# Attention units and projection steps: steps handed out by the units' key blocks instead of by their number

## The chip, the core and the metric

The kernel runs on one core of a Trainium2 chip. The metric is the device time of one execution in microseconds (us); the time before is the median of three runs. A profile is one execution taken by the hardware profiler. TensorE stands in it as PE (matmuls) and PEld (weight loads), VectorE as DVE, ScalarE as ACT, GpSimd as POOL, SyncE, which only issues transfers, as SP.

## The reference

Two decoder layers over 1024 tokens of width 1024, all in float32. Layer 0 mixes with native sparse attention (8 heads in two groups) and differential attention (4 heads, two softmax maps each); layer 1 with stick-breaking attention (16 heads). After each mixer comes an output projection, and then a SwiGLU of hidden width 2816.

```python
o_nsa  = nsa_mixer(q, kc, vc, ks, vs, kw, vw, gates, ...)   # compressed + selected + window, gated
o_diff = diff_mixer(q, k, v, ...)     # (softmax1 - lam * softmax2) @ v, RMSNorm per head
x = x + concat(o_nsa, o_diff) @ w_out;      x = x + swiglu(rmsnorm(x))
# layer 1, strictly causal:
log_rest = where(strict, log_sigmoid(-z), 0);  suffix = cumsum_from_the_right(log_rest) - log_rest
o = exp(log_sigmoid(z) + suffix) @ v;       x = x + o @ w_out;   x = x + swiglu(rmsnorm(x))
out = rmsnorm(x)
```

## The kernel before

Every projection is computed from a high and a low part of both operands, three matmuls for one (mm3, lines 126 to 128). Attention is cut into **units**, each a query block of one head or pair of heads, and a unit into stages s0 (stack the queries), s1 (scores, mask, softmax or scan), s2 (transpose the weights, multiply by the values, store) and, in differential attention, s3 (transpose the result, line 616). `run_segments` pushes the units of a segment one after the other: as unit u comes in, its s0 is written, s1 of the unit before it, s2 of the one before that. Behind each push it writes some **steps** of the projections that the next segment needs. A step is the work up to a generator's `yield`: one token block of a projection (24 matmuls of 256 columns), half a chunk of a query or key projection of layer 1 (12 of 512), or one block of the early output projection (18 of 256). A segment has a number of units, a list of generators, a total of steps n, the number of first units that get none (skip), and in the two last ones a fifth number, 30, over which the steps are spread while n is 1000 (no limit, so what is left goes behind the last unit). Before the change, the steps given out are proportional to the units passed.

The segments: sparse attention group 0 (unit names n0..) with 14 steps, group 1 (n1..) with 17; differential heads d0 to d2 with 9, 17 and 19, and d3 with 30 and four empty units at its end; stick-breaking pairs of heads b0 to b7, eight units each (b712 is pair 7, second head, query blocks 4 and 5; b713 blocks 6 and 7), with 8 steps for even pairs (12 for b6), 16 for odd ones and 30 for b7, which has two empty units at its end. Key blocks of a unit grow with its query block: 1 to 8 in a differential head, 3, 7, 11, 15 in a stick-breaking head, where a unit has two query blocks.

`OutProj.early` writes the output projection of the first six of eight inner blocks during the last segment: per block (oao.. in layer 0, obo.. in layer 1, the digits are column chunk and token block) a read of the residual into a staging tile xr (line 729), 18 matmuls, an add (735) and a write (736). Layer 0 has 8 staging tiles, layer 1 has 4. `late` adds the last two inner blocks (oaq, obq, weights oax, obx) and reads the rows back (750); these rows f0x, f1x go into the norm of the feed-forward (f0n0v, f0n0y and so on, line 180), for which DVE does most of the work. The last head's result reaches the late projection by `put_last` (692, 693).

The program is not executed in the order in which it is written: a scheduler of the build reorders the instructions of each engine by a timeline of its own, within what tiles and pools allow, and each engine then executes its list strictly in that order.

Of the kernel before, what the change touches and what calls it, by code (L numbers as in the profile page):

```python
# [39 lines left out]
def trunk(ctx: ExitStack, tc: tile.TileContext, x, norm_mix, norm_ffn, norm_final,  # L40
# [191 lines left out]
    def run_segments(segs):  # L232
        pend = []

        def push(u):
            pend.append(u)
            for st in range(4):
                for d in range(min(len(pend), 6)):
                    v = pend[-1 - d]
                    if v and v[st] and v[4][st] == d:  # L240
                        v[st]()

        for units, fills, n, skip, *spread in segs:
            work = list(fills)
            taken = 0

            def step():
                while work:
                    try:
                        next(work[0])  # L250
                        return True
                    except StopIteration:
                        work.pop(0)
                return False

            for i, u in enumerate(units):
                push(u)
                want = -(-(spread or [n])[0] * (i + 1 - skip) // max(1, len(units) - skip))
                while taken < want and step():
                    taken += 1  # L260
            while (not units or taken < n) and step():
                taken += 1
        for _ in range(5):
            push(None)
# [5 lines left out]
    def even_attention(op):  # L270
# [220 lines left out]
        def nsa_units(g, q, ks, vs, kw, vw):  # L491
            ap = at_

            def unit(qb, p, box, sel):
                nm = f"n{g}{qb}{p}" + ("s" if sel else "w")
                kb0 = 0 if sel else max(0, qb - 4)
                nk = (qb - kb0 + 1) * 128
# [48 lines left out]
                                                    tmp[:, i * 128:(i + 1) * 128], op=ALU.add)  # L546
                        nc.sync.dma_start(oT_d[g * 2 + p, :, qb * 128:(qb + 1) * 128], os_)

                return s0, s1, s2, None, (0, 1, 2, 3)

            out_ = []
            for qb in range(NT):
                for p in range(2):
                    box = {}
                    out_.append(unit(qb, p, box, False))
                    out_.append(unit(qb, p, box, True))
            return out_

        def diff_units(hd, q, k, v):
            ap = at_  # L560

            def unit(qb):
                nm = f"d{hd}{qb}"
                nk = (qb + 1) * 128
# [56 lines left out]
                    nc.scalar.copy(os_, t[:, :128])  # L621
                    nc.sync.dma_start(oT_d[4 + hd, :, qb * 128:(qb + 1) * 128], os_)

                return s0, s1, s2, s3, (0, 1, 2, 4)

            return [unit(qb) for qb in range(NT)]

        compress()
# [30 lines left out]
        def two(chunk):  # L659
            for _ in range(2):  # L660
                next(chunk)
                yield

        run_segments([
            ([], [fill_kv("ks", [(KS0, 256)], True, lone), fill_kv("kw", [(KW0, 256)], True, lone), two(q0)], 0, 0),
            (nsa(0), [q0, fill_q("q1", NQ0 + 256)], 14, 0),
# [392 lines left out]
    def sb_attention(h, op):  # L1059
        w_in = odd_w_in[0]  # L1060
        with pool("sv", 2) as sv_, pool("sq", 2) as sq, pool("sa", 2) as sa:
# [47 lines left out]
            def unit(i, hh, c):  # L1109
# [63 lines left out]
                    else:  # L1173
                        nc.sync.dma_start(o2T_d[i, pr, c * 256:(c + 1) * 256], tmp[pr])

                return s0, s1, s2, None, (0,1,2,3)

            segs = [([], [v_chunk(0, lone), qk_chunk(0, lone)], 0, 0)]
            xr = []
# [6 lines left out]
            for i in range(8):  # L1186
                units = [unit(i, hh, c) for hh in range(2) for c in range(NT // 2)]
                if i == 7:
                    segs.append((units + [None] * 2, [op.rest(), early], 1000, 2, 30))
                elif i % 2 == 1:  # L1190
                    segs.append((units, [v_chunk((i + 1) // 2), qk_chunk(i + 1)], 16, 2))
                elif i == 6:
                    early = op.early(qk_chunk(i + 1, None, True), 4, stage)
                    segs.append((units, [early], 12, 2))
                else:
                    segs.append((units, [qk_chunk(i + 1)], 8, 2))
            run_segments(segs)

    op = OutProj(oT_d, even_w_out[0], x_d, x1_d, "oa")
# [70 lines left out]
```

## Time and profile before

| | |
|---|---|
| time, median of 3 runs | 2801.74 us (2797.72 to 2805.55) |
| profiled execution: its time, its span | 2809.49 us, 2807.7 us |
| PE busy | 2668.3 us, 95% of the span |
| DVE, ACT, POOL busy | 1880.9, 1244.9, 525.6 us |
| mean granted TensorE clock | 0.981 |

The span runs from the first to the last instruction; the execution's own time is 1.79 us longer. A busy PE counts from issue to modelled end, and matmuls overlap in it. Times in the trace are from the span's start. Attention of layer 0 lies between about 109 and 772 us, its feed-forward until 1460, attention of layer 1 between 1511 and 2110, and then the second feed-forward.

### The profile page before, as it was taken

The numbers are of one execution on the slowest core, as the hardware profiler recorded it, in microseconds if no ns is written. First come the engines' busy times: TensorE is split into PE (matmuls) and PEld (weight loads), VectorE is DVE, ScalarE is ACT, GpSimd is POOL, SyncE is SP. The second block draws the span as 40 slices with busy tenths as digits, with TensorE's granted clock in tenths as the row PEclk, the third lists the DMA queues.
The fourth block names the chain that finished last, engine by engine and source line by source line (L and its number), as shares of the span: only waits on it lengthen the run. The fifth ranks groups of instructions, "written<-read, shape, count | busy, mean of one in ns | idle before, by whom it ended". The sixth has DMA issues, their size and how long they took to land.

```text
span 2807.7 us, 42453 instructions
## 1 busy us (share of the span) xinstructions
PE 2668.3 (95%) x15596; PEld 2307.8 (82%) x15596; DVE 1880.9 (67%) x3266; ACT 1244.9 (44%) x2603; POOL 525.6 (19%) x637
## 2 busy tenths in 40 slices
PE   8999999999979999999999999999887999999998
PEld 7889888898967888888887888787786788888887
DVE  7467667556586666657554767877848657665755
ACT  4366666544353333334443545554425333333433
POOL 3465655444120000000022020211102000000000
PEclk9999999999989999999999999999998999999999
DMA  5100000013445555577643233324434545556754
GB/s 157 32 23 7 23 21 22 23 45 95 123 175 176 150 163 166 159 224 240 198 162 87 59 83 69 94 68 110 124 102 166 174 153 167 160 158 212 256 186 141
DMA packets 327904, 347.70 MB, mean 124 GB/s; under 512 B 24560, under 2 KB 280208, under 8 KB 327696
## 3 DMA queue, kind: packets, MB, share of 16 engines
q1 hardware_dynamic: 327696, 344.98, 40.5%
q8 instruction: 124, 2.03, 0.3%
q14 instruction: 84, 0.69, 0.1%
HBM read 223.79 MB, written 95.94 MB: 114 GB/s over the span
## 4 chain that ended last, share of the span: by engine, by line
PE 69%; DVE 13%; DMA 9%; issue 4%; ACT 4%; POOL 2%; SPq 1%; DVEq 0%; POOLq 0%; ACTq 0%
PE f0o L128 2%; PE f0o L126 2%; PE f0o L127 2%; PE f1o L128 2%; PE f1o L126 2%; PE f1o L127 2%; PE sqo L126 2%; PE sqo L127 2%; PE sqo L128 2%; DMA f1t<-in_ffn_w_down_dram 1%; PE svo L126 1%; PE svo L128 1%; PE svo L127 1%; DMA t_d<-f1t 1%; PE oao L127 1%
## 5 line engine op out<-in xcount | busy, mean ns | idle before, releaser
L113 POOL TENSOR_SCALAR sv0h<-sv0r 128x1024 fp32r<-128x1024 f32 x2 | 2.1, 1057 | 598.9 <-DVE f0c L1043 595.2
L167 POOL TENSOR_TENSOR nf0r<-nf0v,mhalf 128x1 f32<-128x1 f32 x1 | 0.6, 553 | 600.6 <-DVE nf0v L165 600.6
L208 PEld LDWEIGHTS <-ident_b 128*128 128x128 bf16 x352 | 34.2, 97 | 48.2 <-issue 35.7
L1043 DVE TENSOR_TENSOR f1c<-f1o,f1c 128x512 f32<-128x512 f32 x56 | 36.0, 687 | 30.2 <-PE f1o L128 30.1
L1043 DVE TENSOR_TENSOR f0c<-f0o,f0c 128x512 f32<-128x512 f32 x56 | 36.0, 684 | 18.8 <-PE f0o L128 18.8
L951 DVE TENSOR_TENSOR f1t<-f1t 128x256 f32<-128x256 f32 x22 | 9.4, 425 | 51.0 <-DMA f1t<-in_ffn_w_down_dram 51.0
L951 DVE TENSOR_TENSOR f0t<-f0t 128x256 f32<-128x256 f32 x22 | 9.4, 425 | 50.2 <-DMA f0t<-in_ffn_w_down_dram 50.2
L1072 ACT CAST sv<-svo 128x128 fp32r<-128x128 f32 x64 | 17.0, 268 | 48.7 <-PE svo L128 36.3
L1073 DVE TENSOR_TENSOR sv<-svo,sv 128x128 fp32r<-128x128 f32 x64 | 18.2, 286 | 30.0 <-ACT sv L1072 29.8
L702 POOL TENSOR_SCALAR obh<-obr 128x1024 fp32r<-128x1024 f32 (+1 forms) x8 | 12.1, 1530 | 88.8 <-DMA obr<-o2T_d 45.0
L1102 DVE TENSOR_TENSOR kc<-sqo,kc 128x512 fp32r<-128x512 f32 x16 | 11.0, 689 | 23.4 <-ACT kc L1101 23.3
L735 DVE TENSOR_TENSOR xr<-obo,xr 128x256 f32<-128x256 f32 x32 | 13.3, 419 | 18.1 <-PE obo L128 17.9
L735 DVE TENSOR_TENSOR xr<-oao,xr 128x256 f32<-128x256 f32 x32 | 13.3, 419 | 16.6 <-PE oao L128 16.4
L1097 DVE SCALAR_TENSOR_TENSOR qc<-sqo,qc 128x512 fp32r<-128x512 f32 x16 | 11.0, 687 | 18.5 <-ACT qc L1096 18.5
L1101 ACT CAST kc<-sqo 128x512 fp32r<-128x512 f32 x16 | 9.4, 588 | 30.3 <-PE sqo L128 30.3
L126 PE MATMUL cgo<-cgh,hah 128*128 128x280 f32 x64 | 19.7, 309 | 1.7 <-ACT hah L192 1.7
L128 PE MATMUL cgo<-cgh,hal 128*128 128x280 f32 x64 | 20.0, 313 | 0.0
L127 PE MATMUL kso<-ksl,hah 128*128 128x256 f32 x64 | 18.9, 296 | 1.2 <-POOL ksl L115 1.2
L127 PE MATMUL cgo<-cgl,hah 128*128 128x280 f32 x64 | 19.5, 305 | 0.0
L126 PE MATMUL kso<-ksh,hah 128*128 128x256 f32 x64 | 18.6, 294 | 0.9 <-ACT gates L400 0.9
L126 PE MATMUL q0o<-q0h,hah 128*128 128x256 f32 x64 | 19.1, 301 | 0.0
L126 PE MATMUL dk1o<-dk1h,hah 128*128 128x256 f32 x64 | 18.8, 294 | 0.1
(9997 smaller groups left out, 11121.6 us busy)
## 6 DMA issues: line engine op xcount, KB each, us to landing
f0t<-in_ffn_w_down_dram SPq DMA_DIRECT2D x44, 256.0 KB, 3.9
t_d<-f0t SPq DMA_DIRECT2D x22, 512.0 KB, 3.0
f1t<-in_ffn_w_down_dram SPq DMA_DIRECT2D x44, 256.0 KB, 3.9
t_d<-f1t SPq DMA_DIRECT2D x22, 512.0 KB, 2.9
f0dr<-t_d SPq DMA_DIRECT2D x20, 512.0 KB, 4.9
f1dr<-t_d SPq DMA_DIRECT2D x20, 512.0 KB, 5.1
x_d<-xr SPq DMA_DIRECT2D x64, 128.0 KB, 2.3
ks<-kc SPq DMA_DIRECT2D x64, 128.0 KB, 2.3
```

The costliest lines, as they stand in the source:

```text
L126: nc.tensor.matmul(o, a[0], b[0], start=start, stop=False, skip_group_check=onto)
L127: nc.tensor.matmul(o, a[0], b[1], start=False, stop=False, skip_group_check=onto)
L128: nc.tensor.matmul(o, a[1], b[0], start=False, stop=stop, skip_group_check=onto)
L208: nc.tensor.matmul(s[:, b, mo:mo + 128], ident_b, m, start=False, stop=i == len(here) - 1)
L702: nc.gpsimd.tensor_scalar(hs, raw, 1.0, 1.0, op0=ALU.mult, op1=ALU.mult)
L735: nc.vector.tensor_tensor(xr, o[:, :256], xr, op=ALU.add)
L951: nc.vector.tensor_tensor(b11, b12, b11, op=ALU.subtract)
L1043: nc.vector.tensor_tensor(cv, o, cv, op=ALU.add)
L1072: nc.scalar.copy(vs[j][:, tt, :, 0:64], src)
L1073: nc.vector.tensor_tensor(vs[j][:, tt, :, 64:128], src, vs[j][:, tt, :, 0:64].bitcast(F32), op=ALU.subtract)
L1097: nc.vector.scalar_tensor_tensor(lo, o, SCALE, hi.bitcast(F32), op0=ALU.mult, op1=ALU.subtract)
L1102: nc.vector.tensor_tensor(kc[:, 1, :], o, kc[:, 0, :].bitcast(F32), op=ALU.subtract)
```

## The change

A unit now carries its cost, the number of its key blocks, as a sixth entry. Of the steps of a segment, the share given out up to a unit is the share of the costs up to it. The units in skip cost 0, an empty unit costs 2. In sparse attention group 0 every unit costs 4.

```diff
+            cost = [0 if i < skip else u[5] if u else 2 for i, u in enumerate(units)]
             for i, u in enumerate(units):
                 push(u)
-                want = -(-(spread or [n])[0] * (i + 1 - skip) // max(1, len(units) - skip))
+                want = -(-(spread or [n])[0] * sum(cost[:i + 1]) // max(1, sum(cost)))
                 while taken < want and step():
                     taken += 1
...
-                return s0, s1, s2, None, (0, 1, 2, 3)
+                return s0, s1, s2, None, (0, 1, 2, 3), 4 if g == 0 else nk // 128 + (0 if sel else 1)
...
-                return s0, s1, s2, s3, (0, 1, 2, 4)
+                return s0, s1, s2, s3, (0, 1, 2, 4), qb + 1
...
-                return s0, s1, s2, None, (0,1,2,3)
+                return s0, s1, s2, None, (0, 1, 2, 3), 4 * c + 3
```

Worked out from these lines, steps behind each unit as the program is written:

| segment | before | now |
|---|---|---|
| n0 | 14 over 32 units | the same |
| n1, given out after 8, 16, 24, 32 units | 4, 8, 13, 17 | 2, 6, 11, 17 |
| d0 | 0 0 2 1 2 1 2 1 | 0 0 1 1 2 1 2 2 |
| d1 | 0 0 3 3 3 3 3 2 | 0 0 2 2 3 3 3 4 |
| d2 | 0 0 4 3 3 3 3 3 | 0 0 2 3 2 4 4 4 |
| d3 (four empty units last) | 0 0 0 4 3 3 4 3, 3 4 | 0 0 0 4 4 4 6 6, 0 0 |
| b0, b2, b4 | 0 0 2 1 1 2 1 1 | 0 0 2 2 0 1 2 1 |
| b1, b3, b5 | 0 0 3 3 2 3 3 2 | 0 0 3 4 1 2 3 3 |
| b6 | 0 0 2 2 2 2 2 2 | 0 0 3 3 0 1 3 2 |
| b7 (two empty units last) | 0 0 4 4 4 3 4 4, 4 3 | 0 0 5 7 2 3 5 7, 1 0 |

In d3 only 24 steps are left when it starts, so the list above ends where they run out.

What the scheduler makes of it is shown at three places. The first is DVE at the end of d3, where the adds of the early projection end (xr<-oao37), put_last stores the last heads' low parts (oal) and the feed-forward's norm begins (f0x, f0n0v). Before:

```order
L735 TENSOR_TENSOR xr_10140<-oao37_11758,xr_10140 128x256
L693 TENSOR_TENSOR oal11_10135<-d36ot_11779,oah11_10133 128x128
L115 TENSOR_TENSOR oax1l0_11840<-oax1r0_11837,oax1h0_11839 128x1024
L693 TENSOR_TENSOR oal11_10135<-d37ot_11783,oah11_10133 128x128
L766 TENSOR_TENSOR f0x0_11813<-oaq0_11843,f0x0_11813 128x1024
L766 TENSOR_TENSOR f0x4_11814<-oaq4_11857,f0x4_11814 128x1024
L165 TENSOR_SCALAR f0n0v_11959<-f0n0ss_11957 128x1
L180 SCALAR_TENSOR_TENSOR f0n0y_11956<-f0x0_11813,f0n0r_11961,f0g_11821 128x1024
```

Now, from the last softmax combination of d3 (d37p) on; oao37's add and oax1l stand ahead of it:

```order
L586 SCALAR_TENSOR_TENSOR d37p0_11680<-d37p1_11693,d37c2_11700,d37p0_11680 128x1024
L767 TENSOR_TENSOR f0x0_11813<-oaq0_11843,f0x0_11813 128x1024
L165 TENSOR_SCALAR d36v_11729<-d36ss_11726 128x1
L611 TENSOR_TENSOR d36c1_11733<-d36r_11731,d360r_11489 128x1
L612 SCALAR_TENSOR_TENSOR d36on_11724<-d36on_11724,d36c1_11733,sub_150 128x128
L767 TENSOR_TENSOR f0x4_11814<-oaq4_11857,f0x4_11814 128x1024
L694 TENSOR_TENSOR oal11_10204<-d35ot_11775,oah11_10202 128x128
L694 TENSOR_TENSOR oal11_10204<-d36ot_11779,oah11_10202 128x128
L165 TENSOR_SCALAR d37v_11768<-d37ss_11765 128x1
L611 TENSOR_TENSOR d37c1_11772<-d37r_11770,d370r_11685 128x1
L612 SCALAR_TENSOR_TENSOR d37on_11763<-d37on_11763,d37c1_11772,sub_150 128x128
L694 TENSOR_TENSOR oal11_10204<-d37ot_11783,oah11_10202 128x128
```

The next row is f0n0v. The blocks of the early projection, all behind the last unit's work before, now all stand ahead of it, and the last unit's work stands among the first rows of the norm.

The second place is DVE at the end of b7, with the adds of the early projection (xr<-obo), the low parts of the last units' weights (b712pl, b713pl) and of the late projection's weights (obx0l, obx1l). Before:

```order
L735 TENSOR_TENSOR xr_22428<-obo32_23731,xr_22428 128x256
L1156 TENSOR_TENSOR b713pl0_23759<-b713t0_23753,b713ph0_23758 128x512
L115 TENSOR_TENSOR obx0l0_23920<-obx0r0_23917,obx0h0_23919 128x1024
L1156 TENSOR_TENSOR b713pl2_23772<-b713t2_23766,b713ph2_23771 128x512
L1156 TENSOR_TENSOR b713pl4_23785<-b713t4_23779,b713ph4_23784 128x512
L1156 TENSOR_TENSOR b713pl6_23797<-b713t6_23792,b713ph6_23796 128x256
L1170 TENSOR_TENSOR b713ot_23805<-b713o_23752,b713ot_23805 64x256
L735 TENSOR_TENSOR xr_22428<-obo36_23811,xr_22428 128x256
L693 TENSOR_TENSOR obl11_22423<-b713ot_23805,obh11_22421 64x256
L735 TENSOR_TENSOR xr_22428<-obo33_23833,xr_22428 128x256
L735 TENSOR_TENSOR xr_22428<-obo37_23855,xr_22428 128x256
L115 TENSOR_TENSOR obx1l0_23926<-obx1r0_23923,obx1h0_23925 128x1024
```

Now:

```order
L736 TENSOR_TENSOR xr_22428<-obo32_23662,xr_22428 128x256
L736 TENSOR_TENSOR xr_22428<-obo36_23684,xr_22428 128x256
L115 TENSOR_TENSOR obx0l0_23920<-obx0r0_23917,obx0h0_23919 128x1024
L736 TENSOR_TENSOR xr_22428<-obo33_23706,xr_22428 128x256
L1157 TENSOR_TENSOR b712pl0_23758<-b712t0_23752,b712ph0_23757 128x512
L1157 TENSOR_TENSOR b712pl2_23771<-b712t2_23765,b712ph2_23770 128x512
L1157 TENSOR_TENSOR b712pl4_23783<-b712t4_23778,b712ph4_23782 128x256
L736 TENSOR_TENSOR xr_22428<-obo37_23797,xr_22428 128x256
L115 TENSOR_TENSOR obx1l0_23926<-obx1r0_23923,obx1h0_23925 128x1024
L1171 TENSOR_TENSOR b712ot_23791<-b712o_23751,b712ot_23791 64x256
L1157 TENSOR_TENSOR b713pl0_23825<-b713t0_23819,b713ph0_23824 128x512
L1157 TENSOR_TENSOR b713pl2_23838<-b713t2_23832,b713ph2_23837 128x512
```

Both last units have moved behind obo33; before, b712 lay ahead of obo34 and only part of b713 behind obo32.

The third place is DVE in an odd pair, b3, around the last steps of the value projection (sv<-svo); b3..m and b3..e rows are the scan and product of s1, b3..pl rows belong to s2. Before:

```order
L1073 TENSOR_TENSOR sv20_19630<-svo25_19835,sv20_19630 128x2x64
L1133 SCALAR_TENSOR_TENSOR b310m0_20001<-b310m0_20001,zc_95 128x128
L1135 TENSOR_TENSOR b310e0_20000<-b310e0_20000,b310m0_20001 128x127
L1156 TENSOR_TENSOR b302pl0_19898<-b302t0_19892,b302ph0_19897 128x512
L1073 TENSOR_TENSOR sv21_19631<-svo25_19835,sv21_19631 128x2x64
L1133 SCALAR_TENSOR_TENSOR b310m1_20011<-b310m1_20011,zc_95 128x256
L1156 TENSOR_TENSOR b302pl2_19911<-b302t2_19905,b302ph2_19910 128x512
```

Now:

```order
L1074 TENSOR_TENSOR sv20_19630<-svo26_19864,sv20_19630 128x2x64
L1157 TENSOR_TENSOR b302pl0_19927<-b302t0_19921,b302ph0_19926 128x512
L1074 TENSOR_TENSOR sv21_19631<-svo26_19864,sv21_19631 128x2x64
L1157 TENSOR_TENSOR b302pl2_19940<-b302t2_19934,b302ph2_19939 128x512
L1136 TENSOR_TENSOR b312e4_20205<-b312e4_20205,b312m4_20206 128x639
L1157 TENSOR_TENSOR b302pl4_19952<-b302t4_19947,b302ph4_19951 128x256
```

At the values of b302 the scans had reached b310 before and have reached b312 now: the scores run further ahead, as they did in the same piece of b1 already before. In the even pairs b2 and b4, PE's list differs only in where single transposes stand between the matmuls of a step.

## Rows read from the trace of the kernel before

**Rows 1.** The page: busy time of each engine, share of the span, instructions.

```profile
PE 2668.3 (95%) x15596; PEld 2307.8 (82%) x15596; DVE 1880.9 (67%) x3266; ACT 1244.9 (44%) x2603; POOL 525.6 (19%) x637
```

**Rows 2.** Stretches: length, busy PE, PEld, DVE, ACT, POOL, clock, DMA share, GB/s.

```profile
482.00:619.00 137.00, 130.02 (x1044) 121.95 (x1043) 80.68 (x211) 71.67 (x230) 57.89 (x83) 0.99 0.12 35
...
772.00:830.00 58.00, 43.03 (x187) 33.60 (x186) 51.00 (x72) 31.37 (x56) 16.64 (x16) 0.82 0.49 177
...
1588.00:1653.00 65.00, 62.99 (x424) 56.73 (x422) 36.20 (x56) 25.91 (x63) 12.81 (x7) 1.00 0.22 55
1653.00:1720.00 67.00, 61.73 (x377) 51.71 (x376) 58.40 (x80) 42.43 (x91) 9.36 (x6) 0.97 0.43 98
1720.00:1785.00 65.00, 64.81 (x440) 58.74 (x440) 44.31 (x64) 30.31 (x69) 11.96 (x7) 1.00 0.26 63
1785.00:1853.00 68.00, 61.73 (x378) 51.79 (x377) 59.47 (x82) 42.49 (x92) 10.56 (x6) 0.97 0.41 95
...
1918.00:2021.00 103.00, 89.97 (x582) 78.57 (x581) 92.24 (x122) 54.55 (x117) 14.17 (x10) 0.93 0.45 116
2021.00:2110.00 89.00, 78.28 (x591) 74.72 (x590) 46.01 (x73) 20.89 (x44) 10.46 (x8) 0.94 0.37 114
2110.00:2160.00 50.00, 37.00 (x163) 28.54 (x162) 45.15 (x63) 28.50 (x51) 15.76 (x16) 0.80 0.51 192
```

**Rows 3.** The same: early units of n0, the same units of n1, last of n1.

```profile
129.20:152.80 23.60, 20.97 (x162) 18.09 (x161) 14.81 (x58) 13.94 (x49) 13.68 (x26) 1.00 0.02 7
303.30:326.10 22.80, 21.64 (x186) 20.53 (x184) 15.48 (x60) 12.98 (x47) 13.86 (x26) 1.00 0.03 10
447.60:482.00 34.40, 32.15 (x250) 28.57 (x249) 26.90 (x61) 25.16 (x62) 22.66 (x25) 1.00 0.14 37
```

**Rows 4.** Waits of PE, 482 to 619 us: total, times, longest.

```profile
PE d06pt L596 <- DVE d06p L585: 1.3, 1, 1.3
```

**Rows 5.** Waits of PE, 1918 to 2021 us.

```profile
PE b613o L1162 <- DVE b612ot L1170: 2.9, 1, 2.9
PE b602t L1150 <- DVE kc L1102: 2.7, 1, 2.7
```

**Rows 6.** Waits of PE, 2021 to 2110 us.

```profile
PE obq L126 <- POOL obx0h L113: 6.2, 1, 6.2
PE obo L126 <- POOL obw1h L113: 1.1, 1, 1.1
```

**Rows 7.** Timeline of DVE at the end of d3: start, us, what.

```profile
749.51 1.23 DVE L220 TENSOR_REDUCE d371m<-d37s 128x1 f32<-128x1024 f32 x1 [1.42 <-PE d37s L208]
752.72 1.28 DVE L585 SCALAR_TENSOR_TENSOR d37p<-d37p,d37c,d37p 128x1024 f32<-128x1024 f32 x1
...
767.42 0.35 DVE L611 SCALAR_TENSOR_TENSOR d37on<-d37on,d37c,sub 128x128 f32<-128x128 f32 x1
770.96 0.42 DVE L735 TENSOR_TENSOR xr<-oao,xr 128x256 f32<-128x256 f32 x1 [1.74 <-PE oao L128]
...
778.81 1.28 DVE L180 SCALAR_TENSOR_TENSOR f0n0y<-f0x,f0n0r,f0g 128x1024 f32<-128x1024 f32 x1 [0.67 <-POOL f0n0r L167]
```

**Rows 8.** The chain that ended last, 2074 to 2120 us: start, us, what.

```profile
2074.11 0.12 PE obo L128
...
2076.48 2.29 DMA x_d<-xr
...
2079.17 4.04 DMA x_d<-xr
...
2088.85 4.99 DMA obx0r<-in_odd_w_out_dram
2094.01 1.05 POOL obx0h L113
...
2097.82 0.43 PE obq L127
...
2116.27 1.24 DVE f1n0y L180
```

## Prediction

> **What bounds the kernel now.** The page's first part comes first: PE is busy 2668.3 of 2807.7 us [rows 1], so no handing out of its work can win more than its idle time, and only where the segments run. The stretches show how much that is. In d0 to d2 PE idles 137.00 - 130.02 = 7.0 us; in the pair of heads b1 and b2 2.0 and 5.3 us, in b3 and b4 0.2 and 6.3 us; around b6 and the start of b7 13.0 us, over the rest of b7 10.7 us; in the norm between attention and feed-forward 15.0 us after d3 and 13.0 us after b7 [rows 2]. Those two norms are a different case: there DVE is busy 51.0 of 58 and 45.2 of 50 us, so DVE bounds them and PE waits. In b2, b4 and b6 DVE is near its limit too, 58.4 of 67, 59.5 of 68 and 92.2 of 103 us. In b1 and b3 PE is nearly full, and DVE has a third of the time free.
>
> So moving steps helps only where PE now waits for one late result with no step to run. The waits by name show such places: d06's transposes for 1.3 us [rows 4], b602's transposes for 2.7 us and b613's values for 2.9 us [rows 5], and the late projection for the weights obx0, 6.2 us [rows 6]. The chain that ended last says what the last one hangs on: not PE, but SP's list. A write of an early block (issued at 2079.17) lands after 4.04 us, only then come the read behind it, the next write, and obx0's load, issued at 2088.85, landing 4.99 us later, then 1.05 us on POOL [rows 8].
>
> **The change part by part.** The number of instructions hardly changes; work moves. A matmul of 256 columns takes PE 0.12 us when nothing waits [rows 8], so a projection step of 24 is 2.9 us, a step of the early projection 18 x 0.12 = 2.2 us. Each term is the change in time of one place, minus being faster.
>
> *A, group n1.* Halfway, 6 steps are given out where 8 were. Group n0 runs the same units at about that rate: in three early ones PE idles 2.6 us of 23.6, against 1.2 us of 22.8 in the same units of n1 [rows 3]. Over the early half I take +2. The last units, which idle 2.3 us of 34.4, get two more steps; I take -1. Sum +1, bounds -2 (all late idle gone) and +4 (two late steps are 5.8 us, of which some is hidden).
>
> *B, heads d0 to d2.* The last units of a head get one or two steps more and its first ones as many less. d06's wait of 1.3 us should be covered by a whole step of 2.9 us. The first units of the head lose a step; their work is short. I take -1; bounds -4 (most of the 7.0 us of idle) and +3 (a step's length uncovered).
>
> *C, end of d3 and the norm after it.* All early blocks now stand before the last unit's second half. What moves behind the last block, oao37, is d37's last scores, d36's and d37's transposes, values and results: about 55 matmuls at 0.12 us, some 6.5 us. So oao37, whose add is at 770.96 now [rows 7], ends near 764.5. But DVE's new list has the whole end of d37 ahead of f0n0v. From the last scores to the end of d37's softmax it is 754.0 - 749.5 = 4.5 us [rows 7]; then transposes, two copies and values, with a block of oaq between, about 5.9; the head's norm, 2.7 to 3.8; put_last 1; the first norm's own statistics 0.9. That is 15 to 16.5 us from about 765, so f0n0y starts near 780 to 781.5, where it starts at 778.8 now [rows 7]. Behind it DVE has the same work, some 47 us of a stretch in which it has few gaps. I take +1.5. Bounds: -3 if the small gaps of DVE in that stretch close, +6 if the chain of d37 waits once more for DVE's in-order list.
>
> *D, b1 to b5.* The lists of the even pairs hardly change, so their idle should stay. b3 and b5 take the rhythm that b1 had. The pair b1, b2 idles 7.3 us and b3, b4 6.5 [rows 2], so two pairs cost 0.8 each: +1.6, bounds -2 and +4.
>
> *E, b6 and the start of b7.* Two half chunks (5.4 us) stand ahead of b602's transposes where one stood, so its 2.7 us should go. In b7, on the other hand, the last unit of b6 ends one block later in the list, and the weights obw1 are loaded only behind its result; the wait for them, 1.1 us for the high part [rows 6] and as much for the low, grows by one block, 2.2 us. Sum -0.5, bounds -7 (half of the 13.0 us that PE idles there) and +6 (the scores of b603 come a chunk later to a DVE that is full).
>
> *F, end of b7 and the norm after it.* Between the first block of the last column and obx0, six early blocks stand where three or four stood, 13 us of work for PE. It would cover obx0's wait, if SP came as early as now. But each block costs SP a write, its landing and a read: from 2076.48 to 2079.17, 2.7 us [rows 8], against 2.2 us on PE. With blocks following each other closely SP falls behind by 0.5 us a block, 4 us over the eight blocks of a column, and obx0's load is that much later. So I leave most of the 6.2 us. Behind it, obo37 is through before b713's values, so the weights obx1 and the gain of the norm arrive earlier, while b712's and b713's low parts (seven of 0.4 to 0.7 us) now load DVE's list. By the same count as in C, f1n0y starts 2 to 3 us nearer to the column's first block; now it is at 2116.27 [rows 8]. I take -2; bounds -6 (the whole wait) and +5 (SP's lag, and DVE's).
>
> [...]
>
> The sum is +1 - 1 + 1.5 + 1.6 - 0.5 - 2 = +0.6. The execution's own time becomes 2809.49 + 0.6 = 2810.1. That execution was 7.75 us above the median of the three runs, so on their scale the forecast is 2801.74 + 0.6, about **2802 us**. The half widths of the bounds, taken as independent (3, 3.5, 4.5, 3, 6.5, 5.5), give 11 us.
>
> **The rivals.** *The waits are covered (faster).* Everything that PE waits for by name goes: B -4, E -5.6 (b602 and b613), F -6, and in C PE's 6.5 us moved under DVE's work give -3, with A at 0 and D at 0: -18, or 2783; half of it, which I think the likeliest form, gives 2793. For it speaks that PE idles most in the segments of b6 and b7, whose units differ most; against it, that SP and DVE's order, not a lack of steps, end the largest waits.
>
> *The last unit of d3 and of b7 is bare (slower).* The two empty units of b7 get 1 and 0 steps, those of d3 none. DVE executes its list in order, and f0n0v and f1n0v stand behind the last unit's low parts. If that chain starts as late as its last row allows, the norm waits: C +6, F +5, with A +2: +13, or 2815. The point from which it decides: the last put_last row on DVE more than 4 us later, against the last early add, than in my count in C. For it speaks that DVE has no slack in these stretches; against it, that PE reaches that point 6.5 us earlier.
>
> *The clock falls (slower).* In the 6 us wait of 2088.9 PE idles, and right after it a matmul of the late projection takes 0.43 us [rows 8]; the mean clock of the norm behind it is 0.80 [rows 2], so the lower level, 1.2 GHz, is granted for part of it. If the bare ends lengthen such waits by half, some 10 us more at half clock with PE about half busy add 2 to 3 us at each end, on top of F and C at their middle: +8 to +10, or 2811. The Trainium skill ("TensorE: Matmul & The Clock Gate", section "HAM oscillation — how this bites in real kernels") says that waits between bursts of matmuls throttle the engine again; this trace agrees in that stretch.
>
> *The change does nothing (same).* Group n0 is untouched, and the scheduler gives even pairs nearly the old list. If it undoes the rest as well, or the terms cancel, 2802.
>
> **How the numbers follow.** About 0.3%, 8.4 us, is what a measurement can tell here from no change; three runs spread over 7.8 us. My sum and the case of no effect are both inside it: 0.57 together (0.45 and 0.12). The covered waits get 0.23, since PE's idle places are real; the bare ends 0.15 and the clock 0.05, together 0.20. The range goes from half of the covered waits and a little more, 2790, to the bare ends less a little, 2813, which leaves about one in ten on either side.
>
> **What would show it.** In the new trace: d06's wait of 1.3 us gone (B); idle in the early units of n1 near 2.6 us in three of them (A); the last early add of d3 near 764.5 and f0n0y 2 us later than now, both less the shift of what lies before (C); b4's idle near 5.3 and b3's near 2.0 us (D); no wait at b602 (E); PE still waiting 3 to 7 us for obx0 (F). I would be wrong if the waits for obx0 and b613 both vanish, or if DVE waits more than 3 us ahead of f0n0v or f1n0v.

## The result and the profile after

The changed kernel takes 2830.72 us (median of 4 runs, 2829.62 to 2832.95), the kernel before on the same chip 2802.44 (4 runs): ratio 1.0113, 95% interval 1.0099 to 1.0127, 28 us slower. The forecast was 2802 with a range up to 2813, so it was wrong. The profiled execution took 2829.62, 20.1 over the one of before; that one lay 7.0 over its own median.

The page's first part of the changed kernel, and its stretches at the times of [rows 2] and [rows 3] (columns as there):

```profile
PE 2675.2 (95%) x15596; PEld 2312.9 (82%) x15596; DVE 1880.0 (66%) x3266; ACT 1245.6 (44%) x2603; POOL 532.7 (19%) x637
```

```profile
482.00:619.00 137.00, 132.57 (x1074) 125.06 (x1073) 81.67 (x217) 73.64 (x240) 58.82 (x84) 0.99 0.13 36
772.00:830.00 58.00, 39.59 (x183) 31.23 (x182) 47.23 (x72) 31.15 (x60) 18.92 (x17) 0.82 0.41 153
1588.00:1653.00 65.00, 61.42 (x409) 55.62 (x410) 40.26 (x61) 26.85 (x62) 13.87 (x6) 0.97 0.20 50
...
303.30:326.10 22.80, 20.33 (x153) 17.03 (x153) 15.62 (x60) 14.57 (x51) 13.44 (x26) 1.00 0.04 13
447.60:482.00 34.40, 33.01 (x262) 29.92 (x262) 25.45 (x61) 24.04 (x61) 21.95 (x25) 1.00 0.14 37
```

The number of matmuls is the same, yet PE is busy 6.9 us longer [rows 1]. The mean granted clock, 0.980 against 0.981, makes some 3 us of that, an estimate from these figures; the rest is not traced. Up to d2 the picture is as forecast: idle in three early units of n1 rose from 1.2 to 2.5 us, in its last units it fell from 2.3 to 1.4, and in d0 to d2 from 7.0 to 4.4. The stretch after d3 idles 18.4 us instead of 15.0. In b1 idle rose from 2.0 to 3.6, where no loss was expected.

Fixed times mix a shift with a loss. So from here on stretches go from one point of the work to the same point: from the first matmul that bears a head's name (from d3 on, its first scores) to that of the next. That is the start of one row in each trace, and the executions below can be set side by side (us):

| stretch | before | before again | changed | e1 | e2 | e3 | e4 |
|---|---|---|---|---|---|---|---|
| n1, d0 to d2 | 399.5 | 396.9 | 397.4 | 398.9 | 398.5 | 398.0 | 398.3 |
| d3 to the norm's first transposes | 91.5 | 91.5 | 96.4 | 99.6 | 91.5 | 99.2 | 99.9 |
| b0 | 54.4 | 54.2 | 53.8 | 54.2 | 53.9 | 52.3 | 53.9 |
| b1 to b5 | 352.9 | 352.8 | 365.5 | 352.4 | 367.2 | 367.0 | 361.8 |
| b6 to first block with obw1 | 104.4 | 103.9 | 108.7 | 110.2 | 110.3 | 101.8 | 108.0 |
| from there to the second norm's first transposes | 96.1 | 96.0 | 91.9 | 94.2 | 92.3 | 93.6 | 92.9 |

Where a row's handing out is that of before, the entries agree within 3 us, whatever lies ahead of them; where it is changed, within 4. The two feed-forwards are not in the table, since the change leaves them alone: from the first norm's transposes to b0 the 17 executions take 728.0 to 733.0 us, from the second's to the end 682.3 to 692.1.

**b1 to b5.** This is the largest item, and the trace of before already held it. There, from first scores to first scores, b1 takes 87.3 us and b3 80.3, for the same matmuls:

```profile
1565.50:1652.80 87.30, 79.06 (x521) 69.88 (x520) 58.18 (x85) 39.75 (x92) 17.09 (x9) 0.98 0.28 68
1704.90:1785.20 80.30, 77.35 (x523) 69.38 (x521) 57.35 (x83) 41.24 (x94) 13.94 (x8) 0.98 0.32 77
```

The same stretches of b1, b3 and b5 in the changed kernel:

```profile
1569.60:1657.90 88.30, 79.03 (x521) 69.68 (x520) 58.72 (x85) 40.13 (x92) 18.96 (x9) 0.98 0.28 67
1709.30:1796.80 87.50, 79.60 (x522) 70.66 (x522) 58.19 (x84) 41.10 (x94) 16.44 (x8) 0.96 0.30 71
1848.30:1935.10 86.80, 79.42 (x523) 70.55 (x522) 58.23 (x85) 41.11 (x94) 15.63 (x7) 0.96 0.28 65
```

b3 and b5 now take about what b1 took before. Of the 7 us more in b3, 4.95 are idle time of PE (7.90 against 2.95) and 2.25 are PE busy longer at a mean clock of 0.96. The waits of PE in that stretch (total, times, longest):

```profile
PE b213t L1151 <- DVE b212pl L1157: 2.3, 1, 2.3
PE b303t L1151 <- DVE sv L1074: 1.5, 1, 1.5
PE b213t L1151 <- DVE b213pl L1157: 1.5, 1, 1.5
PE b303t L1151 <- DVE b303pl L1157: 1.3, 1, 1.3
PE b300t L1151 <- DVE b213pl L1157: 0.7, 1, 0.7
```

PE waits for low parts on DVE (L1157), at the end of b2's last unit and at b303. DVE's timeline at the first place shows why they are late:

```profile
1719.12 1.49 DVE L1134 TENSOR_TENSOR_SCAN b302m<-b302m,zc 128x640 f32<-128x640 f32 x1
...
1721.46 1.22 DVE L1134 TENSOR_TENSOR_SCAN b301m<-b301m,zc 128x512 f32<-128x512 f32 x1
1722.60 0.66 DVE L1157 TENSOR_TENSOR b213pl<-b213t,b213ph 128x512 fp32r<-128x512 f32 x1
...
1724.94 0.69 DVE L1157 TENSOR_TENSOR b213pl<-b213t,b213ph 128x512 fp32r<-128x512 f32 x1
1725.54 1.75 DVE L1134 TENSOR_TENSOR_SCAN b302m<-b302m,zc 128x768 f32<-128x768 f32 x1
1727.21 2.00 DVE L1134 TENSOR_TENSOR_SCAN b303m<-b303m,zc 128x896 f32<-128x896 f32 x1
1729.12 0.93 DVE L1136 TENSOR_TENSOR b302e<-b302e,b302m 128x767 f32<-128x767 f32 x1
1729.97 0.42 DVE L1157 TENSOR_TENSOR b213pl<-b213t,b213ph 128x256 fp32r<-128x256 f32 x1
```

Scans of the next pair, up to b303's, stand between the low parts of b213; in before the last of these parts starts at 1721.49, behind no scan later than b302's first (1720.09). DVE has no gap here in the changed kernel; it does the same work in an order in which PE's needs come last. In PE's list of the build both scores of b303 have moved ahead of the first step of the value projection; before, 24 matmuls of that projection stood ahead of them. The third list of the section on the change shows the same lead a little later in b3.

**The end of d3.** ACT at the norm's start, and DVE from the late weights on:

```profile
780.78 0.27 ACT L693 CAST oah<-d37ot 128x128 fp32r<-128x128 f32 x1 [1.95 <-PE d37ot L617]
780.94 1.06 ACT L178 ACTIVATE f0n0y<-f0x 128x1024 f32<-128x1024 f32 x1
```

```profile
757.40 1.23 DVE L115 TENSOR_TENSOR oax0l<-oax0r,oax0h 128x1024 fp32r<-128x1024 f32 x1 [5.24 <-POOL oax0h L113]
...
763.63 0.42 DVE L736 TENSOR_TENSOR xr<-oao,xr 128x256 f32<-128x256 f32 x1 [1.73 <-PE oao L128]
...
769.73 1.22 DVE L767 TENSOR_TENSOR f0x<-oaq,f0x 128x1024 f32<-128x1024 f32 x1
...
783.24 1.28 DVE L180 SCALAR_TENSOR_TENSOR f0n0y<-f0x,f0n0r,f0g 128x1024 f32<-128x1024 f32 x1
```

The first row of the norm's input is complete at 770.95, but its statistics on ACT start at 780.94, right behind the last copy of d37: 10 us in ACT's list. In before they started right behind the sum:

```profile
776.80 1.07 ACT L178 ACTIVATE f0n0y<-f0x 128x1024 f32<-128x1024 f32 x1 [4.18 <-DVE f0x L766]
```

From the last early add, 763.63, to f0n0y it is 19.6 us, where before has 7.9 [rows 7]. The early blocks of before were not all behind the last unit's work, as the section on the change has it: the last seven adds came between 754.85 and 770.96 us, among the transposes and values of d37.

**Waits that were to go.** d06's wait of 1.3 us [rows 4] is gone, but d10's scores wait 1.6 us, where before has 0.3. b602's transposes wait 0.6 us instead of 2.7 [rows 5], but b602's values now wait 1.2 and b610's scores 1.0. PE's waits for weights of the projections in b7:

```profile
PE obq L126 <- POOL obx0h L113: 3.8, 1, 3.8
PE obo L126 <- POOL obw1h L113: 3.1, 1, 3.1
```

obx0's fell from 6.2 to 3.8 and obw1's rose from 1.1 to 3.1 [rows 6].

### The profile page after: what moved, and what is told of

The parts are those of the page before. It is cut to its first block, busy times and chain, and to the rows that moved or that the text cites. A ratio compares the mean times of both kernels' runs of the same rounds, so it can differ in the third digit from the quotient of the medians.

```text
span 2827.8 us, 42485 instructions
## 1 busy us (share of the span) xinstructions
PE 2675.2 (95%) x15596; PEld 2312.9 (82%) x15596; DVE 1880.0 (66%) x3266; ACT 1245.6 (44%) x2603; POOL 532.7 (19%) x637
## 5 line engine op out<-in xcount | busy, mean ns | idle before, releaser
L1044 DVE TENSOR_TENSOR f0c<-f0o,f0c 128x512 f32<-128x512 f32 x56 | 35.9, 683 | 18.4 <-PE f0o L128 18.4
L736 DVE TENSOR_TENSOR xr<-oao,xr 128x256 f32<-128x256 f32 x32 | 13.3, 419 | 19.6 <-PE oao L128 19.5
L1097 ACT ACTIVATE qc<-sqo 128x512 fp32r<-128x512 f32 x16 | 9.6, 599 | 37.5 <-PE sqo L128 37.5
L128 PE MATMUL cgo<-cgh,hal 128*128 128x280 f32 x64 | 20.1, 313 | 0.0
L126 PE MATMUL dk3o<-dk3h,hah 128*128 128x256 f32 x64 | 18.8, 293 | 0.3 <-ACT d23qs L468 0.3
```

The source lines that it names most:

```text
L126: nc.tensor.matmul(o, a[0], b[0], start=start, stop=False, skip_group_check=onto)
L128: nc.tensor.matmul(o, a[1], b[0], start=False, stop=stop, skip_group_check=onto)
L736: nc.vector.tensor_tensor(xr, o[:, :256], xr, op=ALU.add)
L1044: nc.vector.tensor_tensor(cv, o, cv, op=ALU.add)
L1097: nc.scalar.mul(hi, o, SCALE)
```

## The experiments

The ratios are against before on the same chip: 2795.87 us for e1 to e4, 2802.37 for e0 and e5 to e7, 2802.03 for e8 to e11, 2800.15 for e13 to e15. The differences from the changed kernel are differences between two such ratios, and their intervals reach 5 to 7 us to either side. **e1 to e4** undo the change in some segments, by one line (seg is the segment's name):

```diff
-            cost = [0 if i < skip else u[5] if u else 2 for i, u in enumerate(units)]
+            cost = [0 if i < skip else 1 if seg in BYNUM else u[5] if u else 2 for i, u in enumerate(units)]
```

BYNUM is b0 to b5 for e1:

> The change everywhere except in the segments of b0 to b5, whose steps go by number as before. Theory 1 (the loss of b1 to b5, 12.9 us between the two traces, comes from how the steps of these very heads are given out): about 13 us under the changed kernel, 2818, and in the trace b1 to b5 take what they took before (b3's pair 133 us, where the changed kernel has 140). Rival (the loss is not theirs, but follows from what lies before them or from the clock): less than 4 us under the changed kernel, 2827 or more, and the waits for b303's and b213's low parts stay.

2815.34 us, ratio 1.0063 (1.0043 to 1.0083): 0.50%, 14 us, under the changed kernel's ratio, and b1 to b5 take 352.4. The loss is these heads' own. e2, BYNUM d3:

> The change everywhere except in d3, whose steps go by number as before. Theory 1 (the bare last unit of d3 holds back the norm behind it by the order of ScalarE's and VectorE's lists, 6.3 us between the traces): 6 us under the changed kernel, 2824.5, and the first norm's statistics on ScalarE start within 2 us of the first add of the late projection. Rival (those 6 us are the norm's own, whose DVE work is the bound in either case, so that a wait of the same size comes later): within 2 us of the changed kernel, 2830.

2821.12, ratio 1.0084 (1.0071 to 1.0097), 0.29% or 8 us less; 91.5 us from d3's scores to the norm, as before, and the statistics again start right behind the sum. e3, BYNUM b6 and b7:

> The change everywhere except in b6 and b7, whose steps go by number as before. By the traces b6 and the start of b7 lost 3.5 us and the end of b7 with the norm won about 2. Theory 1 (both are of these segments): 1 to 2 us under the changed kernel, 2829, with the wait for obx0 back at about 6 us and that for obw1 back at about 1. Rival (b6 inherits what b5 leaves behind, so the 3.5 us stay, and only the gain goes): 2 us over the changed kernel, 2833.

2820.68, ratio 1.0082 (1.0068 to 1.0097): 8.7 us less, where 1 to 2 were expected. Both theories missed, since I had read the shares off one pair of profiles: the table shows that b6 loses 4 to 8 us by the change, and the end of b7 wins nothing sure. The wait for obw1 is back at 0.9 us, that for obx0 is 4.8. e4, BYNUM b1, b3 and b5:

> The change everywhere except in b1, b3 and b5, whose steps go by number as before; b0, b2 and b4 keep it. Two theories share the 12.9 us of b1 to b5. Theory A (the second head's small units in an odd pair get one step less each, and the wait for b303's low parts comes from there): half or more of it back, 2822 to 2824, the wait of 2.85 us at b303's transposes gone, the wait of 3.8 us at b213's transposes still there. Theory B (the even pairs leave their last unit without cover at the change of pair): 2 us back at most, 2829, and both waits stay.

2826.41, ratio 1.0105 (1.0092 to 1.0119), 2 us less, which is within the interval; b3 is at 86.1. So mainly Theory B: most of what b3 pays is decided by the steps of the even pair ahead of it. Not all: b1 to b5 take 361.8 us, 4 to 5 less than where all of them are changed, about a third of their loss. b213's transposes still wait 2.4 and 1.0 us, as B has it, but the 2.8 at b303's transposes have become 1.2 at its values, which is partly A.

**e5 and e8: one step moved, twice.** The kernel before, with a table of steps for b2 and b4 in which a single half chunk changes its unit, one later (e5, the first line) or one earlier (e8, the second):

```diff
+    STEPS = {'b2': [0, 0, 2, 1, 1, 1, 2, 1], 'b4': [0, 0, 2, 1, 1, 1, 2, 1]}
...
+    STEPS = {'b2': [0, 0, 2, 2, 0, 2, 1, 1], 'b4': [0, 0, 2, 2, 0, 2, 1, 1]}
...
+                if seg in STEPS:
+                    want = sum(STEPS[seg][:i + 1])
```

> The kernel before, with one edit: in b2 and b4 one half chunk is given out behind the seventh unit instead of behind the sixth (0 0 2 1 1 1 2 1 for 0 0 2 1 1 2 1 1). In the build's lists this alone puts both scores of b303 and of b503 ahead of the first step of the value projection, as in the changed kernel. Theory B1 (the order at the change of pair, scores ahead of steps, is what b3 and b5 pay for): 5.5 to 7 us each, so 11 to 14 us over before, less what its other list of the second feed-forward saves (about 4), so 7 to 10 us over before, and 87 us from b3's first scores to b4's, where before has 80. Theory B2 (it is the sum of all edits to the steps of b0 to b5 that costs): less than 3 us over before, and 80 to 82 us for b3.

> The kernel before, with one edit of the same size as in the fifth experiment: in b2 and b4 one half chunk is given out one unit earlier (0 0 2 2 0 2 1 1 for 0 0 2 1 1 2 1 1). In the build's lists the value projection stays ahead of b303's scores. Theory B1 (the order of the lists costs, not the number of steps behind a unit): b3 takes 80 to 81 us from its first scores to b4's, and the time is within 3 us of before. Theory B2 (any shift of these steps towards the key blocks costs): 3 us or more a pair, 6 to 12 over before.

e5: 2807.79, ratio 1.0019 (1.0005 to 1.0033); e8: 2798.14, ratio 0.9987 (0.9978 to 0.9995). b3 in e5, then in e8:

```profile
1702.90:1789.20 86.30, 80.11 (x523) 70.82 (x522) 57.54 (x84) 41.05 (x94) 14.47 (x8) 0.96 0.30 72
```

```profile
1700.80:1780.10 79.30, 76.01 (x524) 68.07 (x521) 57.28 (x83) 41.26 (x94) 13.98 (x8) 1.00 0.33 78
```

86.3 and 79.3 us for the same matmuls. Theory B1 holds in its place. In the whole, e5 lost 5 us where 7 to 10 were expected: in its profiled execution b3 and b5 took 6.0 and 4.7 us more than in before, and b1 and the way from b6 to the norm were shorter (85.8 and 198.0), which other executions show too, without this edit. e8 came out 3.6 us under before, a little beyond the 3 us of B1.

**e6, e14: one table, both orders.** b0 alone gets 0 0 1 1 2 2 1 1 (e6); b0, b2 and b4 get it (e14).

```diff
+    STEPS = {'b0': [0, 0, 1, 1, 2, 2, 1, 1]}
```

> The kernel before, with the steps of b0 alone given out as 0 0 1 1 2 2 1 1 instead of 0 0 2 1 1 2 1 1. In the build's lists this puts the value projection's steps ahead of b103's scores, as they are ahead of b303's in before. Theory B1: b1 then takes 80 us from its first scores to b2's, where before has 87, and the time is 5 to 7 us under before. Theory B2 (b1's 87 us are its own, being the first pair after b0's start): b1 keeps 86 to 88, and the time is within 2 us of before.

> The kernel before, with the steps of b0, b2 and b4 given out as 0 0 1 1 2 2 1 1. This is the table that took b1 to 79.7 us in the sixth experiment; in the build's lists it puts steps ahead of the scores of b103, as there, but the scores of b303 and b503 ahead of the steps. Theory B1 (the order of the lists costs): b1 79 to 80 us from its first scores to b2's, b3 and b5 84.5 to 86.5 where before has 80, and 2 to 5 us over before. Theory B2 (the table as such is the better one): all three at 79 to 80, and 6 to 9 us under before.

e6: 2795.09, ratio 0.9973 (0.996 to 0.9986), 7 us under before. e14: 2810.43, ratio 1.0038 (1.0026 to 1.0049). b1, b3 and b5 of e14:

```profile
1564.20:1643.80 79.60, 75.08 (x503) 67.37 (x502) 58.85 (x83) 39.72 (x91) 12.11 (x7) 0.98 0.30 73
1699.80:1784.40 84.60, 78.07 (x508) 68.17 (x507) 58.80 (x84) 40.20 (x92) 12.60 (x7) 0.98 0.29 69
1839.40:1924.10 84.70, 78.18 (x510) 67.99 (x508) 58.79 (x84) 40.23 (x92) 11.87 (x6) 0.98 0.27 63
```

The same table ahead of b1, b3 and b5 gives 79.6, 84.6 and 84.7, each as its list of the build had it. Theory B2 falls. The total missed (11 us over before, 2 to 5 expected): b2 and b4, too, took 4 and 2 us longer than in before (56.0 and 55.0), as did b0 in e6 and e14 (56.2 against 54.4). Part of that is work that moved: b1, b3 and b5 hold 12 to 18 matmuls less than in before (503 to 510 against 521 to 523). Among themselves they hold nearly the same and still lie 5 us apart.

The order can be read from PE's rows in every trace, and it sorts all the odd heads. In the 27 where no matmul of the value projection stands ahead of the first scores of b103, b303 or b503, the head takes 84.6 to 89.5 us; in the 24 where 24 stand ahead, 79.2 to 80.4. Nor is this only the clock: in e8, e10 and e11 all three odd heads ran at 1.00, and b1, with its scores first, took 85.7, b3 and b5 79.2 to 79.3.

**e0, e7, e15.** The kernel before once more, and the combinations:

> All segments by number: the program of the kernel before, executed and profiled once more, to see how far a profile of one program differs from another. Theory 1 (the first profile of before, whose time lay 7.8 us above the median, lost 5 us or so in b6 and b7, where the profile of the third experiment takes 195.4 us from b6's first scores to the second norm against 200.5): b6 and b7 take 195 to 196 us here. Rival (the 5 us are of the order that the third experiment's b5 leaves behind): 200 us again.

> The change in n1 and d0 to d2 only, everything else by number but b0, whose steps are those of the sixth experiment. Theory: the sum of the two gains, 2 us from n1 to d2 (the traces' difference at d3's first scores) and 5 to 7 us from b1, so 7 to 9 us under before. Rival (the gain at d3's start is given back in d3, whose end waits for SyncE's list and not for PE): 5 us under before.

> The sixth and the eighth experiment's edits together: b0 with 0 0 1 1 2 2 1 1, b2 and b4 with 0 0 2 2 0 2 1 1, all else by number. Theory (the 3.6 us that the eighth experiment won are the spread of what follows and not of b2 to b5, which took what they take in before): as the sixth, 6 to 8 us under before. Rival (two gains that add up): 10 to 12 us under before.

e0's profiled execution took 2808.06; b6 to the norm took 199.9 against 200.5, so the rival's number came out. Its reason is not shown: seven later executions with the same steps in b6 and b7 and various lists in b5 took 194.2 to 198.0. e7: 2794.37, ratio 0.9972 (0.9961 to 0.9984), no better than e6; its n1 to d2 took 398.8 us against 396.8 in e6: the change wins nothing there. That its time lies in the theory's range is luck, for e6 alone wins as much. e15: 2792.33, ratio 0.9971 (0.996 to 0.9982), about as e6, so e8's 3.6 us show no sum with it, though the interval, 5 to 11 us under before, reaches into the rival's range. e6, e7 and e15, which share the edit in b0, beat both kernels.

**e10, e11: b6 and b7 apart.** The change in b6 alone (e10) and in b7 alone (e11), by BYNUM for all others.

> The change in b6 alone, all else by number. From b6's first scores to the first block with the weights obw1 the six executions with b6 by number take 101.8 to 104.4 us, the four with the change 108.0 to 110.3. Theory E1 (it is b6's own handing out): 107 to 110 here, and 4 to 6 us over before at the second norm. Rival (it is b7's steps, of which the first go out in fives and sevens, or what b5 leaves behind): 102 to 105, and within 2 us of before.

> The change in b7 alone, all else by number. From the first block with the weights obw1 to the second norm's first transposes the six executions with b7 by number take 90.7 to 96.1 us, the four with the change 91.9 to 94.2. Theory F (six blocks ahead of obx0's load cover half of PE's wait for it, as the prediction had it): 92 to 94.5, and 1 to 3 us under before. Rival (SyncE's chain of write, landing and read gives nothing back): 95 to 97, and within 1 us of before or over it.

e10: 2806.17, ratio 1.0015 (1.0004 to 1.0026), 108.6 us up to obw1: Theory E1. Its waits of PE in b6, to be held against [rows 5]:

```profile
PE obo L126 <- DVE b613pl L1163: 2.6, 1, 2.6
PE obo L126 <- POOL obw1h L113: 2.5, 1, 2.5
PE b700s L205 <- ACT b613e L1138: 1.9, 1, 1.9
...
PE b602o L1169 <- DVE b601ot L1177: 1.2, 1, 1.2
...
PE b602t L1157 <- DVE qc L1104: 1.0, 1, 1.0
```

The two long waits are gone, and others stand in their place: all that the view lists in this stretch sum to 15.2 us, and to 14.2 in before. Of the 4.2 us more than in before (108.6 against 104.4), 1.6 are idle time of PE and 2.6 PE busy longer, at no lower a clock (0.94 against 0.93). DVE is busy 92.90 us, against 92.44 in the same work of before: it has no more to do and idles 3.7 us more, so its load alone is not the reason. PE's rows show one that fits: two half chunks, 48 matmuls, stand between b6's first scores and b603's instead of one, and these come 23.5 us after b6's first scores, against 17.1 in before, e0 and e11. No run tests that alone. Behind b6 the stretch from obw1 on took 92.3 us, so up to the norm e10's profile is no longer than that of before (200.9 against 200.5). e11: 2803.23, ratio 1.0002 (0.9993 to 1.0011), 95.9 us from obw1 to the norm: the rival, nothing is won.

**e9, e13: the end of d3.** Three early blocks behind the last unit instead of seven (e9, the first diff); the changed kernel without the second stage of d37 (e13, the second): its transposes, values and head norm are left out, and d36's result is stored in its place:

```diff
+    STEPS = {'d3': [0, 0, 0, 4, 4, 4, 5, 4, 2, 1, 0, 0]}
```

```diff
                 def s2():
+                    if hd == 3 and qb == 7:
+                        return
...
+                    last_on[hd] = on
...
-                    nc.tensor.transpose(t[:, :128], box["on"], ident)
+                    nc.tensor.transpose(t[:, :128], box.get("on", last_on.get(hd)), ident)
```

> The kernel before, with the early blocks of d3 so given out that three of them stand behind the last unit, where before has seven and the changed kernel none (0 0 0 4 4 4 5 4, 2 1 0 0). From d3's first scores to the norm's first transposes before takes 91.5 us and the four executions with the change 96.4 to 99.9. Theory C1 (each block that is put ahead of the last unit delays that unit's chain, behind which the norm's first rows stand on ScalarE and VectorE): in between, 94 to 97, and 3 to 5 us over before. Rival (the norm is late only where the last unit has no block behind it to hide its chain): 91.5 to 92.5, and no change of the time.

> The changed kernel, with the second stage of d37 left out (its transposes, values and head norm; the result of d36 is stored in its place, so that part of the output is left out). From d3's first scores to the norm's first transposes the executions with the change take 96.4 to 99.9 us, those without 91.5. Theory C1 (the norm's first statistics stand behind d37's last copy in ScalarE's list, and that copy ends the chain of d37): 89 to 92.5, the statistics start within 2 us of the first add of the late projection, and the time is 6 to 9 us under the changed kernel, about 0.8% over before. Rival (the late projection's weights and the rows read back, behind SyncE's list of early blocks, hold the norm): 95 to 99, and the time within 3 us of the changed kernel.

e9: 2810.66, ratio 1.0027 (1.0017 to 1.0037), 98.5 us: as long with three blocks behind as with none. Both theories missed, and this is another loss than that of the changed kernel. The statistics start 0.2 us behind the sum, and f0n0y comes 7.6 us after the last early add, as in before. It is this add that is late, 88.3 us after d3's first scores instead of 80.1:

```profile
776.43 0.42 DVE L742 TENSOR_TENSOR xr<-oao,xr 128x256 f32<-128x256 f32 x1 [0.70 <-PE oao L128]
```

```profile
PE oaq L126 <- POOL oax0h L113: 4.1, 1, 4.1
```

In PE's rows parts of the late projection (oaq) now stand ahead of the last early blocks, and the first of them waits for its weights. So e9 says nothing on how the loss through d37's chain grows. e13: 2829.57, ratio 1.0105 (1.0091 to 1.012), 94.9 us. ACT and DVE of e13:

```profile
778.28 0.27 ACT L698 CAST oah<-d36ot 128x128 fp32r<-128x128 f32 x1 [4.79 <-PE d36ot L622]
...
778.60 1.07 ACT L178 ACTIVATE f0n0y<-f0x 128x1024 f32<-128x1024 f32 x1
```

```profile
773.00 1.22 DVE L772 TENSOR_TENSOR f0x<-oaq,f0x 128x1024 f32<-128x1024 f32 x1
...
782.27 1.28 DVE L180 SCALAR_TENSOR_TENSOR f0n0y<-f0x,f0n0r,f0g 128x1024 f32<-128x1024 f32 x1 [1.29 <-DMA f0g<-in_norm_ffn_dram]
```

The statistics now wait 4.4 us behind the add (774.22 to 778.60) instead of 10, behind d36's copy; from the last early add, 766.82 here, to f0n0y it is 15.5 us instead of 19.6, so the chain of d37 accounts for some 4 us. Then a load holds it: the norm's gain f0g, issued on SP only behind a transfer that needs the first sum. So each theory had a part: 94.9 lies between their ranges, and 3.4 us of the stretch remain over before. The time didn't fall by the expected 6 to 9 us: in this execution b0 to b5 took 424.1 us against 419.3 in the changed kernel's profile. In b1 and b5 that goes with the clock (0.96 and 0.94 against 0.98 and 0.96, 1.2 and 1.6 us longer); the rest is not explained.

## Why the prediction was wrong

The mechanism of lists in strict order was right; sizes were wrong, and all to one side. Each term, with the bounds that it was given and what the stretches show (executions with the change against those by number):

| term | forecast | bounds | measured |
|---|---|---|---|
| A and B, n1 to d2 | +1 - 1 | -6 to +7 | +0.5 to +2.5 (397.4 to 399.3 against 396.8 to 396.9, the first profile of before aside) |
| C, end of d3 | +1.5 | -3 to +6 | +5 to +8 |
| D, b1 to b5 | +1.6 | -2 to +4 | +13 |
| E, b6, start of b7 | -0.5 | -7 to +6 | +6 (108.0 to 110.3 against 101.5 to 104.4) |
| F, end of b7 | -2 | -6 to +5 | about 0 (91.9 to 95.9 against 90.7 to 96.1) |

By the middles that is 1.5 + 6.5 + 13 + 6 = 27 of the 28 us. That it fits so closely is partly luck, for the feed-forwards, which are no term, spread by 5 and 10 us between executions.

**The step that failed is D**, word for word "The pair b1, b2 idles 7.3 us and b3, b4 6.5 [rows 2], so two pairs cost 0.8 each". That b3 and b5 would take over b1's rhythm was right, and e5, e6 and e14 show that this rhythm, not the number of steps, is what costs. Its price was read from windows that start at 1588, 22.5 us behind b1's first scores, and run on into the start of b3, so the start of b1 is not in it. Before's stretch of these 22.5 us, and the same of b3:

```profile
1565.50:1588.00 22.50, 16.27 (x102) 13.36 (x101) 22.09 (x31) 14.05 (x31) 4.48 (x2) 0.92 0.45 103
...
1704.90:1727.40 22.50, 19.74 (x141) 17.79 (x140) 19.24 (x29) 13.96 (x32) 1.78 (x1) 0.92 0.45 103
```

PE idles 6.2 us in the one and 2.8 in the other. These 3.5 us are most of the idle time that b1 has over b3 (8.24 against 2.95); 1.7 more of the 7.0 are PE busy longer. From scores to scores b1 and b2 take 139.3 us and b3 and b4 133.3, so two pairs cost 6.0 each: D would have been +12, and the forecast 2813.

**C** was named rightly and sized too small twice. The blocks were to end 6.5 us earlier after d3's start and ended 1.1 to 4.7 earlier (80.1 us before, 75.4 to 79.0 with the change): oax0l's wait of 5.24 us stands ahead of their adds on DVE. From the last add to f0n0y I had counted 15 to 16.5 us (the parts that I named sum to 15.0 to 16.1), and it took 19.6: 1.6 until d37's last scores are taken up, behind oax1l, which I had not counted; 4.6 for the softmax, as forecast; 8.2 for transposes, copies and values, between which PE runs blocks of oaq, for 5.9; 5.2 for the head's norm, put_last and the statistics, as forecast.

**E** foresaw obw1's longer wait (2.2 us more forecast, 2.0 in the changed kernel) and b602's shorter one. What it kept for its upper bound only, that the scores of b603 come a chunk later, is what the traces show: 22.2 to 23.5 us after b6's first scores in the changed kernel, e4 and e10, 15.9 to 17.1 in before, e0, e3 and e11. That this makes the +6 is argued from the lists. **F** was forecast as a gain that SP's lag would not eat; the wait for obx0 fell, but it was 3.8 and 4.8 us in e8 and e3 too, whose b7 goes by number.

**The rivals.** "Covered waits" had its rows right and fell: waits that DVE's order ends come back elsewhere. "Does nothing" fell. "Bare last units" holds in d3, not in b7; the last put_last row on DVE came 17.5 us after the last early add, 2 to 3 more than in my count, so the point of 4 us from which it was to decide was set too high. "The clock falls" holds in part, not at the norms (0.82 from 772 to 830 us in both kernels) but inside b1 to b5 (below); its own sum was off, since C and F at the middle of their bounds, +1.5 and -0.5, and 2 to 3 us at each end make +5 to +7, not +8 to +10.

**Open**: why the scheduler puts b303's scores first. Which tables tip it can be read from its lists, not why. Open, too, are the odd pairs' own third of D and what of E the later scores of b603 make.

## What to carry to other kernels

Price a pattern from one point of the work to the same point one round later, never between two clock times: here the trace of before held 12 of the 13 us. Where a scheduler writes the lists, an edit's first effect may be that the lists tip into another order: moving one step by one unit was worth 5 to 6 us a head or nothing. Here, work put in front of a wait that another engine's order ended did not cover it: the wait came back at another row.

## What the runs showed of the hardware

In the changed kernel the late order costs clock as well as waits. Granted clock of the changed kernel behind the waits at b213 and at b303:

```profile
1724.00:1728.00 4.00, 3.49 (x15) 3.35 (x16) 3.94 (x5) 1.90 (x4) 0.00 (x0) 0.57 0.09 20
...
1764.00:1768.50 4.50, 1.65 (x13) 1.25 (x12) 4.50 (x8) 2.29 (x5) 4.42 (x2) 1.00 0.36 118
1768.50:1772.00 3.50, 3.50 (x13) 3.02 (x13) 2.75 (x5) 2.12 (x4) 1.08 (x1) 0.52 0.43 111
```

At b303 PE idles 2.85 of 4.50 us at full clock, and then runs 3.5 us without a pause at 0.52, which is about the lower level of 1.2 GHz: about half of those 3.5 us, an estimate from the 0.52, is lost after the wait is over. The Trainium skill ("TensorE: Matmul & The Clock Gate", section "HAM oscillation — how this bites in real kernels") says that waits between bursts throttle the engine again; these rows agree. Not every late order pays it: b3 of e14 has the mean clock of before's, 0.98, and b1 of e8 runs at 1.00.

One list takes longer or shorter with the clock that an execution is granted: b1 as in before takes 87.1 to 87.3 us at a mean of 0.98 (before, e0, e1, e9) and 85.7 to 85.8 at 1.00 (e5, e8, e10, e11).

Where the clock is the same, too, stretches of attention repeat closely: n1 takes 182.9 to 183.0 us in before, e0, e5 and e8, and d3 to the norm 91.5 in before, e0 and e2. Whole executions of one kernel spread by 3 us (e2, 4 runs) to 21 (before, 29 runs, 2794.92 to 2815.84), so for an edit in one place the stretch tells more than the total.
